# Attention of a decoder trunk: from one block after another to a three-step order with pinned runs

## The chip, the cores and the metric

The kernel runs on one core of a Trainium2 chip. A core has five engines with an instruction queue each: TensorE (PE, matrix products; its weight loads are shown apart as PEld), VectorE (DVE), ScalarE (ACT), GpSimd (POOL) and SyncE (SP, which issues most DMA transfers). An engine works through its queue in order and waits on semaphores where an instruction needs another engine's result. The metric is the time of one execution on the device in microseconds (us), as the median over runs.

## What is computed

A trunk of two layers on a sequence of 1024 tokens of width 1024, in float32. Layer 0 mixes with retention and RWKV-7 heads; layer 1 with sliding-window attention; each is followed by a SwiGLU feed-forward net, and a final RMSNorm ends it. The change is in layer 1's attention (16 query heads in 4 groups, 4 key/value heads, window 128, a learned sink per head):

```python
z = h @ w_qkv + b_qkv
q, k, v = jnp.split(z, [SWA_WIDTH, SWA_WIDTH + SWA_KV_HEADS * HEAD_DIM], axis=-1)
kb, vb = with_prev(k), with_prev(v)        # the block before and this one: 256 keys
s = jnp.einsum('bnqhgd,bnkhd->bnhgqk', q, kb) * HEAD_DIM ** -0.5
s = jnp.where(valid, s, -jnp.inf)
m = jnp.maximum(jnp.max(s, axis=-1, keepdims=True), sink)
e = jnp.exp(s - m)
p = e / (jnp.sum(e, axis=-1, keepdims=True) + jnp.exp(sink - m))
o = jnp.einsum('bnhgqk,bnkhd->bnqhgd', p, vb)
return o.reshape(B, T, SWA_WIDTH) @ w_o + b_o
```

Then `h = h + mix`, a norm, and `(silu(n @ w_gate) * (n @ w_up)) @ w_down`.

## The kernel before

Activations lie transposed: 128 channels on the partitions, tokens along the free axis. The 1024 tokens are two halves of 512 (`hf` 0 and 1); a half is four blocks of 128 tokens. A large product is made from numbers split into a rounded part and its remainder, `hi` and `lo`: three matmuls for each 128x128 weight tile and 512 columns (hi x hi, hi x lo, lo x hi; lines L350 to L352 in `gemm`, L1182 to L1184 in `prod`). `wload` loads a weight (SP queue), ScalarE casts the `hi` part (L335), and VectorE or GpSimd, whichever `K.lo` names at that moment, makes the `lo` part (L336). Split weights lie in a ring of six tiles, each for four of the eight contraction steps; raw weights in a ring of two (`wr`).

Attention of layer 1, for each half:

- `proj` makes 128 channels of queries, keys or values: eight contraction steps, 24 matmuls, into a bank of the PSUM tag `f` (three banks). VectorE scales by the norm's factor (L1496), ScalarE adds the bias (L1497). `kv` calls it four times and copies the keys with their 64-row halves swapped by DMA (`ks`); `queries` calls it four times for each half of the heads.
- `attn` walks 16 blocks, four groups `g` by four token blocks `b`. For a block, `scores` makes four heads' scores of 128 queries by 256 keys: float32 matmuls on 64 rows (L1562), those of two heads side by side on the two halves of the rows, into the tags `r` and `c`. VectorE adds the mask (L1570), takes the maximum (L1576) and does small steps (L1578 to L1580, L1586, L1587); ScalarE takes the exponentials with their sums (L1583); the four heads are scaled by the reciprocal, three on VectorE (L1592), one on ScalarE (L1590).
- `turn` transposes the probabilities with eight 128x128 matmuls against the identity (L1602, tag `m`, two banks); ScalarE and VectorE copy them out (L1604, L1606).
- `out` multiplies by the values: matmuls with 64 columns, two side by side (L1616, tag `y`, one bank). ScalarE and VectorE write `hi` and `lo` parts (L1625, L1626).
- `w_o` is the output projection: eight times 24 matmuls, added to the residual `h` by VectorE (L1642).

The first block of the first half has no block of keys before it, so its scores, transposes and outputs are half as many or half as long, for each of the four groups.

Around it: `norm` of a half is needed for its projections. After `w_o` of the first half, `factor_of` (squares on ScalarE, sums on VectorE, a matmul L373, Ln and Exp) and `form0` (L1130, L358) make the first operands of the feed-forward net, and `ffn_early` makes first products of the gate and up weights for a pair `p` of channel tiles: 48 matmuls, then Silu (L1237) and a product (L1241); its results go to memory by the SP queue (L1246, L1265).

The program is traced in Python in one order; a planner then makes each engine's queue. It simulates the program's time and takes, for a free engine, the ready instruction that was traced first. So later work moves ahead where earlier work isn't ready. Two calls restrict it: `keep(i)` puts an instruction behind the one traced just before it on the same engine; `behind(i, first)` puts it behind a named one. The order of the queues is then fixed. In the kernel before, `attn` uses neither:

```python
for j in range(len(blocks)):
    scores(j, False)
    turn(j)
    out(j, False)
```

and the calls follow as: norm of half 0, keys, values and all queries of half 0; norm of half 1; attention of half 0; keys, values and first queries of half 1; `w_o` of half 0; `form0`; the other queries of half 1; attention of half 1; five pairs of `ffn_early`; `w_o` of half 1. What really interleaves is the planner's choice.

## Time and profile before

| | us |
|---|---|
| three runs, median (lowest to highest) | 2348.12 (2346.57 to 2348.34) |
| the profiled execution, its own time | 2351.35 |
| its span, first to last instruction | 2349.6 |
| first score to last output of both halves | 1432.8 to 1717 in the span |

The granted clock of TensorE was 0.991 on average. In a row of the profile stand the line of the kernel, the engine, the operation, output and inputs by tile name, shapes and a count; then busy time, mean duration, and the idle time ahead of it with what ended it. In a table by stage, each engine has its busy time and in brackets the number of its instructions; then come the clock, the share of DMA and GB/s. A timeline row gives start, duration, engine, line and operation. A float32 matmul is recorded as two instructions, so a block has eight records of scores, eight of transposes and eight of outputs. Busy time of TensorE is modelled from pipelined matmuls; the time between two starts is the surer reading.

### The profile page before, as it was taken

The page shows a single profiled execution, that of the slowest core. Times are in us where ns is not written, and L with a number is a line of the kernel's source. Part 1 is how long each engine was busy: PE and PEld are TensorE (multiplying, and loading weights), DVE is VectorE, ACT ScalarE, POOL GpSimd, SP SyncE. Part 2 cuts the span into 40 slices and gives each one's busy share as a digit, 9 for nine tenths or more (in the row PEclk, how much of TensorE's full clock was granted, in tenths as well). Part 3 has the DMA queues.
Part 4 walks back from the last instruction along what each step waited for, and adds up shares of the span by engine and source line. Part 5 has one row for each costly group of instructions (what it writes and reads, how often), then busy time and mean ns, then how long its engine had stood idle before and what let it go on. Part 6 is the DMA issues. An engine that isn't in the chain of part 4 may idle for free.

```text
span 2349.6 us, 35675 instructions
## 1 busy us (share of the span) xinstructions
PE 2301.8 (98%) x13056; PEld 1822.8 (78%) x13056; DVE 1703.8 (73%) x2667; ACT 1055.7 (45%) x1953; POOL 976.7 (42%) x764
## 2 busy tenths in 40 slices
PE   8999999999999999999999999999999999999998
PEld 6777777777777888888788887777688888887886
DVE  6876765866557548888876876887747788888767
ACT  5354533323555433333333455666735333333335
POOL 3122121211343057777677600002201677776775
PEclk9999999999999999999999999999999999999999
DMA  7565554443345645665685332123236566556763
GB/s 274 199 208 178 180 156 133 131 126 115 126 166 173 208 156 201 216 217 199 231 299 202 126 119 73 51 69 112 93 114 227 172 210 220 212 202 256 257 215 112
DMA packets 170622, 407.46 MB, mean 173 GB/s; under 512 B 43216, under 2 KB 45904, under 8 KB 170448
## 3 DMA queue, kind: packets, MB, share of 16 engines
q1 hardware_dynamic: 167040, 398.63, 49.5%
q10 hardware_dynamic: 2832, 4.45, 0.5%
q8 instruction: 104, 1.70, 0.3%
q0 software_dynamic: 576, 2.10, 0.2%
q14 instruction: 70, 0.57, 0.1%
HBM read 276.53 MB, written 123.21 MB: 170 GB/s over the span
## 4 chain that ended last, share of the span: by engine, by line
PE 75%; DVE 10%; ACT 4%; DMA 4%; issue 4%; POOL 2%; SPq 1%; DVEq 0%; ACTq 0%; POOLq 0%
PE ps_m L1182 7%; PE ps_m L1184 7%; PE ps_m L1183 7%; PE ps_f L240 7%; PE ps_m L240 5%; PE ps_f L350 4%; PE ps_f L352 4%; PE ps_f L351 4%; PE ps_f L1184 4%; PE ps_f L1183 4%; PE ps_f L1182 4%; PE ps_r L1182 2%; PE ps_r L1184 2%; PE ps_r L1183 2%; PE ps_c L1184 2%
## 5 line engine op out<-in xcount | busy, mean ns | idle before, releaser
L240 PE MATMUL ps_f<-n,w 128*128 128x512 f32 x1440 | 387.1, 416 | 10.4 <-ACT w L335 5.7
L240 PEld LDWEIGHTS ps_f<-n,w 128*128 128x128 f32 x1440 | 269.8, 193 | 95.3 <-issue 24.6
L336 POOL TENSOR_TENSOR w<-wr,w 128x512 fp32r<-128x512 f32 x63 | 86.7, 1384 | 524.3 <-ACT w L335 520.6
L335 ACT CAST w<-wr 128x512 fp32r<-128x512 f32 x231 | 141.1, 617 | 181.2 <-PE ps_f L352 70.3
L336 DVE TENSOR_TENSOR w<-wr,w 128x512 fp32r<-128x512 f32 x168 | 119.9, 717 | 56.8 <-ACT w L335 56.3
L336 POOL TENSOR_TENSOR w<-wq,w 128x512 fp32r<-128x512 f32 x91 | 130.4, 1444 | 31.4 <-ACT w L335 31.4
L1182 PE MATMUL ps_m<-n,w 128*128 128x512 f32 x333 | 130.7, 393 | 0.0
L1184 PE MATMUL ps_m<-n,w 128*128 128x512 f32 x333 | 129.8, 390 | 0.4 <-POOL w L1370 0.4
L1183 PE MATMUL ps_m<-n,w 128*128 128x512 f32 x333 | 129.6, 389 | 0.0
L352 PE MATMUL ps_f<-n,w 128*128 128x512 f32 x320 | 126.9, 397 | 0.6 <-POOL w L336 0.6
L350 PE MATMUL ps_f<-n,w 128*128 128x512 f32 x320 | 127.3, 399 | 0.1
L351 PE MATMUL ps_f<-n,w 128*128 128x512 f32 x320 | 126.9, 396 | 0.0
L1191 DVE TENSOR_TENSOR nq<-ps_m,u 128x512 f32<-128x512 f32 x88 | 58.8, 683 | 92.2 <-PE ps_m L1184 92.1
L1182 PE MATMUL ps_f<-n,w 128*128 128x512 f32 x287 | 113.9, 397 | 1.6 <-ACT u L1341 1.6
L1184 PE MATMUL ps_f<-n,w 128*128 128x512 f32 x287 | 112.1, 392 | 0.0
L1183 PE MATMUL ps_f<-n,w 128*128 128x512 f32 x287 | 111.8, 389 | 0.0
L358 POOL TENSOR_TENSOR n<-nq,n 128x512 fp32r<-128x512 f32 x60 | 100.0, 1679 | 7.6 <-ACT n L356 7.6
L1370 POOL TENSOR_TENSOR w<-wd,w 128x512 fp32r<-128x512 f32 (+1 forms) x62 | 85.9, 1393 | 39.6 <-ACT w L1369 37.9
L1182 PE MATMUL ps_m<-cb,w 128*128 128x512 f32 x236 | 91.9, 390 | 0.3 <-DVE nq L1191 0.3
L1183 PE MATMUL ps_m<-cb,w 128*128 128x512 f32 x236 | 91.8, 389 | 0.0
L1184 PE MATMUL ps_m<-cb,w 128*128 128x512 f32 x236 | 91.8, 389 | 0.0
L1370 POOL TENSOR_TENSOR w<-ws,w 128x512 fp32r<-128x512 f32 (+1 forms) x48 | 71.3, 1491 | 47.0 <-ACT w L1369 43.5
(520 smaller groups left out, 6472.9 us busy)
## 6 DMA issues: line engine op xcount, KB each, us to landing
hc<-n SPq DMA_DIRECT2D x84, 512.0 KB, 2.9
wsp<-w SPq DMA_DIRECT2D x54, 512.0 KB, 3.4
w<-wsp SPq DMA_DIRECT2D x54, 512.0 KB, 3.7
n<-hc SPq DMA_DIRECT2D x54, 512.0 KB, 5.7
wq<-in_w_gate SPq DMA_DIRECT2D x44, 512.0 KB, 4.4
u<-u SPq DMA_DIRECT2D x88, 256.0 KB, 2.9
wr<-in_w_in SPq DMA_DIRECT2D x34, 512.0 KB, 5.2
ha<-hc SPq DMA_DIRECT2D x34, 512.0 KB, 5.6
```

The lines of the kernel that those rows point to most:

```text
L240: self.nc.tensor.matmul(out, lhsT, rhs, **kw)
L335: nc.scalar.copy(hi[:, :n], raw[:, c])
L336: self.lo.tensor_tensor(out=lo[:, :n], in0=raw[:, c], in1=hi.bitcast(F32)[:, :n], op=ALU.subtract)
L350: nc.tensor.matmul(ps, hi, rh, start=k == 0, stop=False)
L351: nc.tensor.matmul(ps, hi, rl, start=False, stop=False)
L352: nc.tensor.matmul(ps, lo, rh, start=False, stop=k == n - 1)
L358: e.tensor_tensor(out=lo, in0=src, in1=hi.bitcast(F32), op=ALU.subtract)
L1182: mm(ps, hi, xh, start=first and k == 0, stop=False, skip_group_check=True)
L1183: mm(ps, hi, xl, start=False, stop=False, skip_group_check=True)
L1184: mm(ps, lo, xh, start=False, stop=last and k == len(w) - 1, skip_group_check=True)
L1191: self.last_add = V.tensor_tensor(out=o, in0=x, in1=y, op=ALU.add)
L1370: nc.gpsimd.tensor_tensor(out=lo, in0=v, in1=hi.bitcast(F32), op=ALU.subtract)
```

## The change

`attn` becomes a generator of 19 steps. Step `j` holds the transposes of block j-2, the outputs of block j-3 and the scores of block j, in this order; outputs and scores are each kept behind the matmul traced before, from the point where three blocks are on the way. Behind the scores come the step's fills, whose first matmul is put behind the last matmul of the step before. A fill is a half of a projection (12 matmuls), as `proj`, `kv` and `queries` now yield after four of the eight contraction steps; in the second half it is a half of a gate/up pair (24 matmuls). The first scaling of the four heads goes from VectorE to GpSimd.

The order of calls: only four of half 0's query projections precede its attention; the other four fill steps 0 to 2, half 1's keys and values steps 3 to 8, and five of half 1's query projections steps 9 to 17. Then come the first two steps of half 1's attention, `w_o` of half 0, its third step, `form0`, half 1's last three query projections, and the other steps with the five gate/up pairs as fills.

```diff
+    def pinned(self, x):
+        if self.pin is not None:
+            self.behind(x, self.pin)
+            self.pin = None
...
     def proj(self, nr, ti, out, **kw):
...
-        self.gemm(ps, w, nr[0])
+        for k in (0, 4):
+            self.prod(ps, w[k : k + 4], nr[0][k : k + 4], k == 0, k == 4)
+            if k == 0:
+                yield
...
-                    V.tensor_scalar(
+                    (nc.gpsimd if h == 0 else V).tensor_scalar(
...
-        for j in range(len(blocks)):
-            scores(j, False)
-            turn(j)
-            out(j, False)
-        return [self.hl(n8, k) for k in range(KT)]
+        n = len(blocks)
+        for j in range(n + 3):
+            if 0 <= j - 2 < n:
+                turn(j - 2)
+            if 0 <= j - 3 < n:
+                n8 = n8 or outs()
+                out(j - 3, j - 2 < n)
+            if j < n:
+                scores(j, j >= 3)
+            for f in fill.get(j, ()):
+                self.pin = last
+                f()
+                self.pin = None
+            last = self.tail
+            self.ch[hf] = n8 and [self.hl(n8, k) for k in range(KT)]
+            yield
...
-        kv = K.kv(0, n0, ap)
-        q = [x for j in range(2) for x in K.queries(n0, ap, j)]
+        run(K.kv(0, n0, ap))
+        q0 = K.queries(0, n0, ap)
+        for _ in range(8):
+            next(q0)
         n1 = K.norm(K.kt(K.h[1]), "n1b", K.n8(nb), ap)
-        c0 = K.attn(0, kv, q, ap, K.n8(K.pp))
-        kv = K.kv(1, n1, ap)
-        q = K.queries(n1, ap, 0)
-        K.w_o(0, c0)
+        kv, q1 = K.kv(1, n1, ap), K.queries(1, n1, ap)
...
+        fill = {j: [take(q0)] * n for j, n in enumerate((4, 2, 2))}
+        fill |= {j + 3: [take(kv)] * n for j, n in enumerate((1, 1, 2, 1, 1, 2))}
+        fill |= {j + 9: [take(q1)] * n for j, n in enumerate((1, 1, 1, 1, 1, 2, 1, 1, 1))}
...
+        g = pairs()
+        run(K.attn(0, ap, lambda: K.n8(K.pp), fill))
+        a1 = K.attn(1, ap, lambda: K.n8(nb), {j: [take(g)] for j in (4, 5, 6, 8, 9, 10, 12, 13, 14, 16)})
+        next(a1)
+        next(a1)
+        K.w_o(0, K.ch[0])
+        next(a1)
         gs, sp = K.pool("sp", "left")
         K.form0("n2b", K.factor_of(0, sp), K.n8(K.pp), sp)
-        q += K.queries(n1, ap, 1)
-        c1 = K.attn(1, kv, q, ap, K.n8(nb))
-        K.lo = tc.nc.gpsimd
-        early(1, sp, 0, 5)
+        run(q1)
+        run(a1)
         K.lo = tc.nc.vector
-        K.w_o(1, c1)
+        K.w_o(1, K.ch[1])
```

`gemm` and `prod` call `pinned` on their first matmul; `pairs()` yields each gate/up pair in two halves, with `K.lo` on GpSimd while a pair's weights are split; `ffn_early` yields between its halves.

More of the change, by code (lines that the diff above doesn't have):

```diff
@@ L1181, in prod @@
         for k, ((hi, lo), (xh, xl)) in enumerate(zip(w, x)):
-            mm(ps, hi, xh, start=first and k == 0, stop=False, skip_group_check=True)
+            i = mm(ps, hi, xh, start=first and k == 0, stop=False, skip_group_check=True)
+            self.pinned(i)
             mm(ps, hi, xl, start=False, stop=False, skip_group_check=True)
@@ L1514, in kv @@
             ks.append(st)
[L1515 removed]
+            yield
         if hf:
[L1517 to L1521 removed]
+            G.tensor_copy(vt[:, 0, :], pvt[:, 4, :])
+        for i in range(2):
+            vc = self.t(self.pp, [P, HT], "nq", 4)
+            yield from self.proj(nr, 10 + i, vc, bias=self.col("bqkv", 10 + i))
             pt = self.pst("m", [P, 4, P])
@@ L1746, in early @@
                 K.lo = tc.nc.vector if form else tc.nc.gpsimd
-                K.ffn_early(L, p, sp, "ff" if L and p < 6 else "fm")
+                run(K.ffn_early(L, p, sp, "ff" if L and p < 6 else "fm"))
                 K.lo = tc.nc.gpsimd
```

62 lines of the change are left out of this document (40 added, 22 removed).

## The prediction

> **What bounds the kernel now.** I read the page first: engines, clock, the chain that ended last.
>
> ```profile
> span 2349.6 us, 35675 instructions
> PE 2301.8 (98%) x13056; PEld 1822.8 (78%) x13056; DVE 1703.8 (73%) x2667; ACT 1055.7 (45%) x1953; POOL 976.7 (42%) x764
> PEclk9999999999999999999999999999999999999999
> PE 75%; DVE 10%; ACT 4%; DMA 4%; issue 4%; POOL 2%; SPq 1%; DVEq 0%; ACTq 0%; POOLq 0%
> ```
>
> TensorE (PE) is busy in 98% of the span and the clock never drops, so only PE time can be won. But the page says that ends of matmuls are modelled: a busy PE can still issue late. So the second view is a table by stage, with instructions counted (the number after x), for the four stages around the change: first half's attention, its output projection, second half's attention, its output projection. The same table for scores (L1562), transposes (L1602) and outputs (L1616) follows, for the two attention stages.
>
> ```profile
> 1432.00:1560.00 128.00, 126.47 (x700) 87.52 (x699) 109.51 (x287) 88.44 (x271) 0.00 (x0) 1.00 0.15 47
> 1560.00:1610.00 50.00, 50.00 (x221) 40.76 (x221) 36.61 (x67) 28.15 (x57) 5.46 (x4) 1.00 0.38 131
> 1610.00:1718.00 108.00, 106.51 (x579) 76.12 (x580) 73.32 (x156) 68.81 (x177) 22.02 (x17) 1.00 0.28 99
> 1718.00:1762.00 44.00, 44.00 (x196) 36.40 (x195) 19.96 (x29) 16.01 (x27) 5.16 (x4) 1.00 0.32 108
> ...
> 1432.00:1560.00 128.00, 29.66 (x176) 17.51 (x176) 1.00 0.15 47
> 1610.00:1718.00 108.00, 13.40 (x80) 8.05 (x80) 1.00 0.28 99
> ...
> 1432.00:1560.00 128.00, 21.10 (x136) 15.61 (x136) 1.00 0.15 47
> 1610.00:1718.00 108.00, 16.60 (x104) 11.86 (x104) 1.00 0.28 99
> ...
> 1432.00:1560.00 128.00, 15.84 (x112) 6.53 (x112) 1.00 0.15 47
> 1610.00:1718.00 108.00, 17.24 (x128) 7.65 (x128) 1.00 0.28 99
> ```
>
> The projection stages run at 44/196 = 50/221 = 0.225 us per matmul; with an instruction counted at each edge I use 0.226. The third view is the timeline of PE around one block (start, duration).
>
> ```profile
> 1498.54 0.60 PE L1602 MATMUL ps_m<-c_ident,s 128*128 128x128 f32 x4
> ...
> 1500.13 0.40 PE L350 MATMUL ps_f<-n,w 128*128 128x512 f32 x1
> 1500.46 1.08 PE L1616 MATMUL ps_y<-pT,vt 128*64 128x256 f32 x8
> 1501.47 0.48 PE L1562 MATMUL ps_c<-ks,q 64*128 64x256 f32 x1
> ...
> 1501.79 0.38 PE L1562 MATMUL ps_c<-ks,q 64*128 64x256 f32 x1
> ...
> 1502.01 0.38 PE L1562 MATMUL ps_c<-ks,q 64*128 64x256 f32 x1
> ...
> 1502.53 0.50 PE L351 MATMUL ps_f<-n,w 128*128 128x512 f32 x1
> 1502.87 0.40 PE L352 MATMUL ps_f<-n,w 128*128 128x512 f32 x1
> ```
>
> Scores and outputs run as pairs side by side, a pair per 0.215 us (1501.79 to 1502.01; I take the same for outputs), so four pairs of either need 0.86 us. A transpose takes (0.60 - 0.28)/3 = 0.107 us (0.28 is one's own length). From the matmul at 1500.13 to the one at 1502.87 there are 2.74 us, for 0.226 + 0.86 + 0.86 + 0.226 = 2.17 of work. The other 0.57 go to three changes of form (128x128 to 64 columns, to 64 rows, and back): **0.19 us per change**.
>
> Now the loss by stage. First half: 700 instructions less 176, 136, 112, eight transposes of values and two of a norm leave 266 full matmuls, 60.1 us; scores 72 x 0.215 + 16 half-long pairs x 0.12 = 17.4; 144 transposes 15.4; outputs 56 x 0.215 = 12.0; norm 0.9. That is 105.8 of 128: 22.2 lost. Second half: 267 x 0.226 + 40 x 0.215 + 104 x 0.107 + 64 x 0.215 = 93.8 of 108: 14.2 lost. Together **36.4 us** are lost, and next to nothing elsewhere in the four stages.
>
> Following the timeline between the first score and the last output, I count 42 runs of scores and 33 of outputs (for 32 blocks), nine directly behind one another, and 141 changes of form.
>
> ```profile
> L1562 PE MATMUL ps_c<-ks,q x64: 272/376/480, 1432.8 to 1646.8; 64*128 64x256 f32 x56, 64*128 64x128 f32 x8
> L1616 PE MATMUL ps_y<-pT,vt x240: 379/379/431, 1448.4 to 1717.0; 128*64 128x256 f32 x120
> L1590 ACT ACTIVATE s<-s,st x32: 399/508/517, 1439.6 to 1691.4; 128x256 f32<-128x256 f32 x28, 128x128 f32<-128x128 f32 x4
> 1512.89 0.49 ACT L1590 ACTIVATE s<-s,st 128x256 f32<-128x256 f32 x1
> ...
> 1676.49 0.70 PE L1562 MATMUL ps_c<-kc,q 64*128 64x256 f32 x2
> ```
>
> 141 x 0.19 = 26.8 us. The remaining **9.6 us** I read as waits, mostly on the softmax.
>
> **The change part by part.**
>
> *Pinned runs (gain 7.4).* In each half 16 blocks take 19 steps. Steps 0 and 1 have scores alone (2 changes each), step 2 transposes and scores (2), steps 3 to 15 all three (3 each), steps 16 to 18 outputs at most (2 each): 4 + 2 + 39 + 6 = 51, so 102 for both halves, 19.4 us against 26.8. Lower bound of the gain: if fills fall between outputs and scores, 64 runs make 128 changes, 24.3 us, gain 2.5. Transposes may mix with full matmuls at no cost: they have the same form.
>
> *The wait that the pin adds.* Transposes of block j stand two steps behind its scores, and behind them on PE are queued outputs, scores and the next fill. A full step of the first half is 0.86 + 0.86 + 0.86 + 0.57 = 3.15 us plus 16 fills of twelve matmuls (2.71) over 13 steps, 3.34: 6.49. Scores start about 1.96 (transposes, outputs, two changes) after the step, so the softmax has 2 x 6.49 - 1.96 = 11.0 us. Today it takes, from the first score to the last scaling, 1513.4 - 1501.5 = 11.9 for that block and 1440.0 - 1432.8 = 7.2 for the first (half as long, alone). At 11.9 a step becomes 6.93 and 13 steps lose 5.7; near 7 they lose nothing. In the second half ten fills of 24 matmuls (5.42) make the step 7.32 and leave 12.7; the last block there takes 1691.9 - 1676.5 = 15.4, which would make it 8.68 and lose 17.7. There the softmaxes ran one behind the other, so much of the 15.4 is queueing that later scores would remove. So waits lie between 0 and 23.4 us. I take 5, near the low end, because the 11.9 misses its allowance by under 1 us, fills not pinned behind this step's scores can go ahead of late transposes, and weights of the next fills are split ahead. Against today's 9.6 this gains 4.6.
>
> *One of three scalings to GpSimd.*
>
> ```profile
> L1592 DVE TENSOR_SCALAR s<-s,st 128x256 f32<-128x256 f32 (+1 forms) x96 | 30.3, 371 | 0.2
> L1517 POOL COPY vt<-vt 128x256 f32<-128x256 f32 x1 | 0.6, 622 | 15.3 <-ACT vt L1525 15.3
> 1636.75 1.92 DVE L1592 TENSOR_SCALAR s<-s,st 128x256 f32<-128x256 f32 x3
> 1637.25 1.27 POOL L336 TENSOR_TENSOR w<-wr,w 128x512 fp32r<-128x512 f32 x1 [4.27 <-ACT w L335]
> ```
>
> VectorE loses 30.3/3 = 10.1 us of work; GpSimd gains 32 x 0.62 (its copy of the same shape) = 20, on an engine that did nothing in the first half and 22 of 108 us in the second. It is on no path if it runs beside the other two. The last two rows say it may not: three scalings took 1.92 us while GpSimd worked 1.27, where three alone take 3 x 0.316 = 0.95 (30.3/96 each). Bounds on the softmax: 0.3 shorter to 0.62 + 0.63 - 0.95 = 0.3 longer, or longer still behind a 1.27 us split; I take no change.
> The Trainium skill, "SBUF — State Buffer", section "Who interferes with whom", says that a tensor_scalar on VectorE can hold the port pair that it shares with GpSimd, and that the one that comes second is blocked for the whole instruction. The 1.92 us agrees. By it the sum would be 0.3/2 x 13 = 2 us less gain in the first half; by the row of two engines side by side, none.
>
> *Fills in halves, moves.* The number of matmuls, weight loads and their DMAs is unchanged; only places change. The first half's last four query projections, the second half's keys and values and five of its eight query projections go into the first half's steps; five gate/up pairs into the second's.
>
> ```profile
> L336 DVE TENSOR_TENSOR w<-wr,w 128x512 fp32r<-128x512 f32 x29 | 19.9, 686 | 12.3 <-ACT w L335 12.2
> wr<-in_w_qkv SPq DMA_DIRECT2D x14, 512.0 KB, 3.3
> SPq L1246 <- DVE sg L1241: 54.6, 5, 14.0
> L1130 DVE SCALAR_TENSOR_TENSOR u<-h,pv,rs 128x512 f32<-128x512 f32 x8 | 6.6, 870 | 4.0 <-ACT rs L375 4.0
> L358 DVE TENSOR_TENSOR n<-u,n 128x512 fp32r<-128x512 f32 x8 | 8.3, 1072 | 0.0
> L1237 ACT ACT_TABLE_LOAD x4 | 5.1, 1283 | 0.1
> ```
>
> A fill brings VectorE one split (0.69) ahead of time; its cover is the ring of six weight tiles. Without it each late split costs up to 0.69 us. Loads land in 3.3 us and a fill comes every 3 to 6, but the SP queue is in order and has stood up to 14.0 us behind a pair's write; six tiles are six fills, over 16 us, so I cost it at nothing. The second keys' swapped copy waits in that queue for the first half's scores; its readers come after the output projection. The pairs' activations alternate with exponentials: up to ten table loads where the stage has four and three back, three more, 3.9 us on ScalarE, which is busy 68.8 of 108: hidden; if not, 3.9 on the path.
> Second half's first scores ahead of the output projection: nothing on PE itself. But behind that projection the norm's chain and 8 x (0.87 + 1.07) = 15.5 us on VectorE must pass before the first pair; with the chain I put it at 20. The cover is the six remaining fills (16.3), step 2 (about 2.3) and step 3 (3.15), 21.7: nothing, and up to 4 where softmaxes come between. It is inside the waits' bounds.
>
> **Sum.** 36.4 - 19.4 - 5 = 12.0 us gained. Against the profiled execution's own 2351.35 us this is 2339.4; that run lies 3.2 above the median 2348.12, so against the median it is **2336**.
>
> **Rivals.** *Full gain.* The softmax fits everywhere and waits vanish: gain 17.0, 2331. For it: VectorE still had 18 us idle of 128. Against: VectorE is at 86% there and the order is fixed ahead of time.
> *The softmax distance (slower).* The two steps between a block's scores and its transposes are too short for the softmax, and PE waits the whole 23.4: 36.4 - 19.4 - 23.4 = -6.4, 2354.5. It decides above 17.0 us of waits, that is about 0.65 us in each of 26 full steps. For it: 15.4 us of the last block, and VectorE's in-order waits. Against: fills enough to cover, 11.9 in the first half.
> *It does not do what it says.* The planner that orders instructions puts halves of fills between outputs and scores (only scores and outputs are pinned to what is traced before them, and fills only behind the last step): 128 changes and waits as now, gain 2.5, 2345.6. For it: today's order splits 32 blocks into 75 runs. Against: the pins leave it few places.
>
> **How the numbers follow.** Forecast (2332.5 to 2343) 0.49, full gain 0.18, not doing it 0.13, softmax distance 0.20. What a measurement can tell from no change is 0.2%, 4.7 us. Faster is forecast and full gain, 0.67; same 0.13; slower 0.20. The range goes from 2330, just below the full gain, to 2354, where half of the slower case is left out.
>
> **What would show it.** Right: the two attention stages with the same instructions lose some 24 us in place of 36; scores directly behind outputs in 26 blocks, hence 64 runs and about 102 changes; PE rows of the timeline never further apart than 0.5 us; L1592 twice on VectorE and once on GpSimd per block. Wrong: waits of the transposes on the last scaling (VectorE, GpSimd or ScalarE) of 0.65 us and more at each step, GpSimd's scaling over 1 us, TensorE waiting for a weight split in a fill, or a hole before the first gate/up pair.

## The result, and the profile after

The changed kernel takes 2344.47 us (median of 22 runs, 2338.92 to 2350.74) where the kernel before takes 2348.61 (22 runs, 2344.42 to 2354.38). The ratio is 0.9981, with a 95% interval of 0.9974 to 0.9989: a gain of 4.4 us (2.6 to 6.1). It is real, since the interval leaves out 1, and it lies at the bound of 0.2% that the prediction set for no change. The forecast was a gain of 12.0.

The page of the changed kernel, its span, busy times and the engines of the chain that ended last:

```profile
span 2343.4 us, 35741 instructions
PE 2290.0 (98%) x13056; PEld 1817.0 (78%) x13056; DVE 1697.9 (72%) x2635; ACT 1060.1 (45%) x1956; POOL 1004.2 (43%) x796
...
PE 76%; DVE 10%; ACT 5%; DMA 4%; issue 3%; SPq 1%; POOL 1%; DVEq 0%; ACTq 0%; POOLq 0%
```

TensorE is the bound as before, with the same 13056 matmuls. The profiled run took 2345.18 us; the spans differ by 6.2 us. From the timeline, TensorE's 7100th instruction (first layer, ahead of the stages in question) starts at 1028.4 us before and at 1025.6 after; from there to the 11000th it takes 837.8 and 832.5. So 2.8 us of the 6.2 come from stages that the change does not touch and are no part of its effect, 5.3 come from the stages that it does touch, and 1.9 are lost again behind them. The granted clock of TensorE differs outside these stages: ahead of 1028 us it stood at one half for 34.1 us in the trace before and 20.5 after, and behind them the changed kernel has 3.4 us of it at 2129.6 where the kernel before has none. Between 1372 and 1772 us neither has any.

The stretch from 1372 to 1772 us holds both attention stages and both output projections in either kernel. The table by stage has, after the window and its length, the busy time and the count (x) of TensorE, its weight loads, VectorE, ScalarE and GpSimd, then the granted clock, the DMA share and GB/s. Before:

```profile
1372.00:1772.00 400.00, 396.98 (x2000) 298.38 (x1999) 273.86 (x590) 239.90 (x588) 33.84 (x27) 1.00 0.28 93
```

After:

```profile
1372.00:1772.00 400.00, 394.13 (x2023) 300.37 (x2022) 272.09 (x567) 246.35 (x598) 63.36 (x59) 1.00 0.29 96
```

What counts is x: 23 more matmuls in the same 400 us, although "busy" fell from 396.98 to 394.13. In either kernel 758 instructions of the stretch are the same: 256 scores (25.8 us by their spacing in the timeline), 240 attention transposes (26.1), 240 outputs (25.6), 16 transposes of values (1.7) and 6 of the norm (2.6), together 81.8; two more are cut by the edges, and the rest are full matmuls at 0.2267. So the loss of the stretch (its length less this work) is close to 400 - 81.8 - (x - 760) x 0.2267; counted from the timeline it is 37.0 us before and 31.8 after. The gain there is 5.2.

From the timeline I count in this stretch the changes of form (as the prediction did: between 128x128 matmuls, those on 64 rows and those with 64 columns), and as waits all that a start comes later than is usual for its pair of kinds, where that is over 0.06 us. The kernels of the study by the same count (o_price, which adds work, is told below):

| kernel | changes of form | runs of scores / outputs | waits, us | loss, us | median, us | ratio to before (95%) |
|---|---|---|---|---|---|---|
| before | 141 | 42 / 33 | 5.4 | 37.0 | 2348.61 | 1 |
| after | 108 | 35 / 32 | 7.9 | 31.8 | 2344.47 | 0.9981 (0.9974-0.9989) |
| a_dve | 109 | 36 / 32 | 10.7 | 35.3 | 2345.70 | 0.9991 (0.9980-1.0002) |
| b_bank | 105 | 34 / 32 | 13.2 | 39.6 | 2353.47 | 1.0019 (1.0008-1.0030) |
| c_both | 102 | 32 / 32 | 12.0 | 36.6 | 2345.68 | 0.9989 (0.9978-1.0001) |
| d_between | 125 | 32 / 32 | 50.1 | 77.3 | 2388.09 | 1.0170 (1.0156-1.0184) |
| e_old_pool | 156 | 51 / 33 | 3.0 | 37.2 | 2351.69 | 1.0017 (1.0007-1.0028) |
| f_nopin | 147 | 50 / 37 | 2.3 | 38.3 | 2350.99 | 1.0017 (1.0007-1.0028) |
| g_dist3 | 119 | 38 / 32 | 13.4 | 40.4 | 2352.33 | 1.0023 (1.0013-1.0034) |
| h_pair | 94 | 36 / 18 | 12.0 | 36.4 | 2348.09 | 0.9998 (0.9985-1.0010) |
| k_runs | 104 | 35 / 31 | 10.1 | 33.5 | 2343.51 | 0.9981 (0.9971-0.9992) |
| l_fills | 144 | 43 / 41 | 1.7 | 37.2 | 2350.10 | 1.0006 (0.9995-1.0017) |
| n_pairruns | 99 | 40 / 17 | 3.7 | 29.1 | 2341.70 | 0.9970 (0.9958-0.9981) |

In six of these kernels the granted clock stood at one half for a part of the stretch, and their loss, in part also their waits, holds what that cost, estimated as half of TensorE's busy time there: a_dve, c_both and h_pair 1.7 us each (3.4 us of half clock), b_bank 3.0 (6.8), g_dist3 6.5 (13.7), d_between 17.8 (41.0). The other seven have none.

Changes fell by 33. What is left of the loss once the waits are taken off is 31.6 / 141 = 0.224 us per change before and 23.9 / 108 = 0.221 after. The loss thus splits into 7.7 us won on changes and 2.5 us given back in waits. Over all thirteen kernels the same remainder is 0.22 to 0.26 us per change, so the split holds to a few us and no better.

The timeline of the changed kernel around one step (start, duration, engine and line; in brackets the idle time and what ended it):

```profile
1496.58 0.39 PE L1191 MATMUL ps_f<-n,wx 128*128 128x512 f32 x1
...
1498.00 1.09 PE L1621 MATMUL ps_m<-c_ident,s 128*128 128x128 f32 x8 [1.03 <-POOL s L1611]
1499.02 1.08 PE L1635 MATMUL ps_y<-pT,vt 128*64 128x256 f32 x8
1500.04 0.37 PE L1580 MATMUL ps_c<-kc,q 64*128 64x128 f32 x1
...
1500.68 0.50 PE L1188 MATMUL ps_f<-n,wx 128*128 128x512 f32 x1
```

Both halves of the result stand here. Transposes, eight outputs and eight scores come in one run, as the change says, with three changes of form. And the first transpose starts 1.42 us after a matmul that holds TensorE for 0.23: a wait of 1.19, which the view puts down to GpSimd's scaling.

That scaling did end last, at 1497.94, but VectorE's two of the same block ended only 0.3 us sooner, at 1497.63. All of them started late, since VectorE came late to the reciprocal that they need:

```profile
1495.39 0.16 DVE L1605 TENSOR_TENSOR st<-st 128x4 f32<-128x4 f32 x1
1495.47 1.21 DVE L1595 TENSOR_REDUCE st<-s 128x4 f32<-128x1024 f32 x1
1496.60 0.17 DVE L1606 RECIPROCAL st<-st 128x4 f32<-128x4 f32 x1
```

Between the sum (L1605) and the reciprocal (L1606) of the block that TensorE waits for stands the maximum of the next block (L1595). From sum to reciprocal it is 1.21 us, where it is 0.20 with nothing in between. Something stands there in 13 of the 32 blocks, 0.86 us on average; at the other wait put down to GpSimd (1630.7) it is 0.69. The softmax of this block took 12.2 us from its first score (1485.78), 1.2 more than the 11.0 that the prediction allowed. No run changed VectorE's order alone, so what this order is worth is not shown.

TensorE's waits in the stretch as the profile attributes them (tile and line that waited, what it waited for, us, times, longest). Before:

```profile
PE ps_c L1562 <- DVE st L1586: 1.1, 1, 1.1
PE ps_y L1616 <- DVE n L1626: 0.7, 2, 0.6
PE ps_m L1602 <- ACT s L1583: 0.5, 1, 0.5
PE ps_r L1562 <- DVE s L1570: 0.4, 1, 0.4
```

After:

```profile
PE ps_m L1621 <- ACT vt L1541: 2.1, 2, 1.3
PE ps_m L1621 <- POOL s L1611: 2.1, 2, 1.0
PE ps_m L1621 <- ACT pT L1623: 0.6, 1, 0.6
PE ps_m L1621 <- DVE pT L1625: 0.4, 1, 0.4
PE ps_m L1621 <- ACT s L1609: 0.4, 1, 0.4
PE ps_m L1621 <- DVE s L1611: 0.2, 1, 0.2
```

2.7 us became 5.8 (this view counts only time in which the engine is idle, so it is lower than my count; the difference, 3.1 against 2.5, is much the same). And they moved: before, scores and outputs waited for the most part (2.2 of 2.7); after, all waits are those of the transposes (L1621): 2.7 on the scalings and 3.1 on a free bank (copies of values, L1541, and of transposed probabilities, L1623 and L1625).

### The profile page after: what moved, and what is told of

Same layout as the page of the kernel before. It is cut to its first block, busy times and chain, and to the rows that moved or that the text cites. A ratio compares the mean times of both kernels' runs of the same rounds, so it can differ in the third digit from the quotient of the medians.

```text
span 2343.4 us, 35741 instructions
## 1 busy us (share of the span) xinstructions
PE 2290.0 (98%) x13056; PEld 1817.0 (78%) x13056; DVE 1697.9 (72%) x2635; ACT 1060.1 (45%) x1956; POOL 1004.2 (43%) x796
## 4 chain that ended last, share of the span: by engine, by line
PE 76%; DVE 10%; ACT 5%; DMA 4%; issue 3%; SPq 1%; POOL 1%; DVEq 0%; ACTq 0%; POOLq 0%
PE ps_f L240 8%; PE ps_m L1188 7%; PE ps_m L1191 7%; PE ps_m L1190 7%; PE ps_f L1188 5%; PE ps_f L1190 5%; PE ps_m L240 5%; PE ps_f L1191 5%; PE ps_r L1188 2%; PE ps_r L1190 2%; PE ps_r L1191 2%; PE ps_c L1191 2%; PE ps_c L1190 2%; PE ps_c L1188 2%; PE ps_f L353 2%
## 5 line engine op out<-in xcount | busy, mean ns | idle before, releaser
L240 PE MATMUL ps_f<-n,w 128*128 128x512 f32 x1440 | 384.4, 414 | 10.1 <-ACT w L335 6.1
L240 PEld LDWEIGHTS ps_f<-n,w 128*128 128x128 f32 x1440 | 267.5, 191 | 94.4 <-issue 23.6
L1188 PE MATMUL ps_f<-n,w 128*128 128x512 f32 x415 | 164.8, 397 | 1.6 <-ACT u L1349 1.6
L1190 PE MATMUL ps_f<-n,w 128*128 128x512 f32 x415 | 163.3, 393 | 0.1
L1191 PE MATMUL ps_f<-n,w 128*128 128x512 f32 x415 | 162.4, 392 | 0.0
L1611 POOL TENSOR_SCALAR s<-s,st 128x256 f32<-128x256 f32 (+1 forms) x32 | 30.1, 942 | 208.5 <-DVE st L1606 55.6
L1378 POOL TENSOR_TENSOR w<-wd,w 128x512 fp32r<-128x512 f32 (+1 forms) x62 | 86.0, 1394 | 40.4 <-ACT w L1377 37.0
L1188 PEld LDWEIGHTS ps_f<-n,w 128*128 128x128 f32 x415 | 77.8, 188 | 23.0 <-issue 4.7
L1190 PEld LDWEIGHTS ps_f<-n,w 128*128 128x128 f32 x415 | 77.9, 188 | 19.1 <-issue 2.9
```

What stands on the lines that cost most here:

```text
L240: self.nc.tensor.matmul(out, lhsT, rhs, **kw)
L1188: i = mm(ps, hi, xh, start=first and k == 0, stop=False, skip_group_check=True)
L1190: mm(ps, hi, xl, start=False, stop=False, skip_group_check=True)
L1191: mm(ps, lo, xh, start=False, stop=last and k == len(w) - 1, skip_group_check=True)
L1378: nc.gpsimd.tensor_tensor(out=lo, in0=v, in1=hi.bitcast(F32), op=ALU.subtract)
L1611: (nc.gpsimd if h == 0 else V).tensor_scalar(out=s[:, h, kw], in0=s[:, h, kw], scalar1=den[:, h : h + 1], scalar2=None, op0=ALU.mult)
```

## Experiments

The theory in the end: the gain is the changes of form, at about 0.2 us each, and most of the rest of the forecast was lost because pinned runs make TensorE stand still where before another instruction went first. Its rivals: one late supplier (GpSimd's slow scaling, or the bank) makes the new waits, and with it gone the forecast's gain comes; the two steps between scores and transposes are too few; changes of form are worth little, and both the loss and the gain are waits.

### One late supplier: a_dve, b_bank, c_both

a_dve has all scalings that are not ScalarE's on VectorE:

```
-                    (nc.gpsimd if h == 0 else V).tensor_scalar(
+                    V.tensor_scalar(
```

> The changed kernel with all three scalings back on VectorE. My theory now: in the two attention stages TensorE loses 31.8 us, 108 changes of form at 0.22 and 7.9 us of waits; 2.4 of these are transposes waiting for GpSimd's scaling (1.19 at 1496.6, 1.18 at 1629.3), because one takes 0.94 us there against 0.42 on VectorE. Then the loss falls to about 29.4 and the time by 2 us against the changed kernel. Rival: GpSimd relieves VectorE, which gets 10 us of work back; the softmax grows longer, waits stay at 8 us or grow, and the time is the same or up to 3 us longer.

b_bank turns the values in the projections' banks, so that the transposes of the attention do not wait for the copy of the values:

```
-            pt = self.pst("m", [P, 4, P])
+            pt = self.pst("f", [P, 4, P])
```

> The changed kernel with the four value transposes of each half's second fills in a bank of the three-bank tag f in place of the two-bank tag m. My theory: the waits of 1.44 at 1470.3 and 1.03 at 1477.7 are attention transposes for which no bank of m is free until ScalarE, behind four exponentials, has copied the values out; without them the loss falls by 2.5 to 29.3 and the time by 2.5 us. Rival: the softmax of that block isn't ready any sooner, and the wait comes back under another name: loss 31 to 32, time the same.

c_both has both edits.

> Both edits: scalings on VectorE and value transposes in the other tag. If the two waits are independent: loss 31.8 - 4.9 = 26.9, time 5 us below the changed kernel and 9 to 10 below the kernel before (ratio 0.996). If waits only change their names: loss about 31, time as the changed kernel.

The table by stage of a_dve:

```profile
1372.00:1772.00 400.00, 393.21 (x2008) 298.67 (x2007) 272.06 (x592) 244.56 (x595) 33.25 (x27) 1.00 0.28 95
```

Of b_bank:

```profile
1372.00:1772.00 400.00, 388.16 (x1988) 295.93 (x1988) 266.88 (x555) 240.87 (x589) 63.83 (x59) 0.99 0.28 92
```

Neither gains: 2008 and 1988 matmuls against the 2023 of the changed kernel, and c_both has 1999. TensorE's waits of c_both show why:

```profile
PE ps_m L1621 <- DVE s L1611: 3.7, 4, 1.4
PE ps_f L1540 <- ACT nq L1510: 3.4, 2, 1.9
PE ps_f L1188 <- ACT u L1349: 1.0, 1, 1.0
PE ps_f L350 <- ACT sg L1244: 1.0, 1, 1.0
PE ps_m L1621 <- ACT s L1609: 0.8, 1, 0.8
PE ps_m L1621 <- DVE pT L1625: 0.7, 1, 0.7
```

The wait for the copy of the values is gone, and so is GpSimd's; in their place the value transposes wait for their own operand (L1540), full matmuls for theirs, and the same transposes for VectorE's scaling. c_both even reaches the 102 changes of the forecast and has 12.0 us of waits. The rival of one late supplier falls in this form: the waits for each are in the list of the changed kernel, but with a supplier taken away TensorE waits elsewhere. Since an edit makes the planner place every later instruction anew, these runs do not say what one wait alone would be worth.

### Where the fills stand: d_between

The fills stand between a step's outputs and its scores, which costs one change of form more in each step:

```
-            if j < n:
-                scores(j, j >= 3)
+            if j < 3:
+                scores(j, False)
             for f in fill.get(j, ()):
-                self.pin = last
+                self.pin = self.tail if j >= 3 else last
                 f()
                 self.pin = None
+            if 3 <= j < n:
+                scores(j, True)
```

> The changed kernel with the fills of steps 3 to 15 put between outputs and scores in place of behind the scores: nothing is added but changes of form, one more pair of changes less one joint in each of 26 steps, 26 changes. My theory, 0.22 us per change: loss 31.8 + 5.7 = 37.5, time 5.7 us longer than the changed kernel, slower than the kernel before by 1. Rival: the stages are bound by the softmax and the changes of form are in the shadow of its waits: loss and time within 1.5 us of the changed kernel.

Measured: 125 changes, 17 more than the changed kernel, and 2388.09 us, 44 more. At 0.22 the changes are 3.7 us. The count of gaps rose from 7.9 to 50.1, but not all of that is waits: the profile lists 31.5 us of them (5.8 in the changed kernel), and about 18 are the half clock behind the longer ones, which stood for 41.0 us of the stretch. The first row of TensorE's waits of this kernel:

```profile
PE ps_m L1621 <- POOL s L1611: 20.9, 7, 5.1
```

The table by stage:

```profile
1372.00:1772.00 400.00, 368.57 (x1823) 272.12 (x1822) 245.35 (x528) 223.91 (x559) 58.54 (x55) 0.95 0.24 79
```

With the fills between outputs and scores, a step's scores come directly ahead of the next step's transposes. That does two things at once: nothing is left to work on when the transposes are late, and the softmax, which starts at the scores, has the length of a fill less time (2.7 or 5.4 us by the prediction's sizes). The run does not tell these apart. Either way a fill's place behind the scores is worth far more than the change of form that it saves, and the expectation, which priced little more than the changes, missed it.

### Which pin does it: f_nopin, k_runs, l_fills

The changed kernel has two kinds of pins: scores and outputs held in the order in which they are written (the runs), and a step's fills held behind the last run. f_nopin has neither, k_runs the first alone, l_fills the second alone:

```
f_nopin:
-                out(j - 3, j - 2 < n)
+                out(j - 3, False)
...
-                scores(j, j >= 3)
+                scores(j, False)
...
-                self.pin = last
+                self.pin = None
k_runs:
-                self.pin = last
+                self.pin = None
l_fills:
-                out(j - 3, j - 2 < n)
+                out(j - 3, False)
...
-                scores(j, j >= 3)
+                scores(j, False)
```

> The changed kernel's steps, fills and order of calls, but nothing pinned. In its queue of TensorE the two attention stages have 147 changes of form (changed kernel 108, before 141). Theory of the changes at 0.22 us: loss 147 x 0.22 = 32.3 and waits as in the changed kernel, 7.9: 40 in place of 31.8, time 8 us above the changed kernel, ratio to the kernel before about 1.001. Rival: the pins are what makes TensorE wait; free of them it waits 5 us or less and gives back part: loss 37, time 5 above. Second rival, the order of steps and fills is what gained and the pins nothing: time as the changed kernel.

> The changed kernel with the runs pinned (outputs behind transposes, scores behind outputs) and the fills free. 104 changes of form in the queue. Without any pin the two stages lost 147 x 0.22 and 2.3 us of waits; with both pins 108 x 0.22 and 7.9. If the run's pin makes the waits (TensorE stands before a transpose with outputs, scores and next fills queued behind it): waits of 6 to 10, loss 29 to 33, time within 2 us of the changed kernel, ratio to before 0.9970 to 0.9990. If the fills' pin makes them: waits of 2 to 4, loss 26, time 6 us below the changed kernel, ratio 0.9955.

> The changed kernel with the fills pinned behind the last step and the runs free. 144 changes of form in the queue. If the run's pin makes the waits: waits of 2 to 4, loss 144 x 0.22 + 3 = 35, time 3 us above the changed kernel. If the fills' pin makes them: waits of 6 to 8, loss 39, time 7 us above it, ratio to before 1.001.

The tables by stage; f_nopin:

```profile
1372.00:1772.00 400.00, 398.71 (x1994) 298.20 (x1993) 265.01 (x557) 242.17 (x591) 63.38 (x59) 1.00 0.27 93
```

k_runs:

```profile
1372.00:1772.00 400.00, 391.04 (x2015) 299.45 (x2014) 273.15 (x568) 244.97 (x596) 64.32 (x59) 1.00 0.28 95
```

l_fills:

```profile
1372.00:1772.00 400.00, 398.78 (x1999) 297.39 (x1998) 265.02 (x557) 243.06 (x592) 62.93 (x59) 1.00 0.28 94
```

TensorE's waits of f_nopin, all of them:

```profile
PE ps_y L1635 <- DVE n L1646: 0.7, 1, 0.7
PE ps_f L1188 <- ACT u L1349: 0.4, 1, 0.4
PE ps_f L1190 <- DVE n L364: 0.2, 1, 0.2
```

Of k_runs, its three longest:

```profile
PE ps_m L1621 <- POOL s L1611: 2.9, 4, 1.1
PE ps_f L350 <- ACT n L1645: 2.1, 2, 1.6
PE ps_m L1621 <- ACT pT L1623: 1.3, 1, 1.3
```

The four kernels make a square. Pinning the runs takes 43 changes away without the fills' pin (147 to 104) and 36 with it (144 to 108), and adds 7.8 and 6.2 us of waits (2.3 to 10.1, 1.7 to 7.9). It makes both, the gain and the new waits: outside the waits the loss falls by 12.6 and 11.6 us, the waits take back 7.8 and 6.2, and the net is 4.8 and 5.4 us of loss. (43 and 36 changes at 0.2 are only 8.6 and 7.2; what the other 4 us are was not found.) The pin of the fills does nothing here that can be told: 0.9981 with and without it, and 1.0006 against 1.0017 with overlapping intervals. And the new order of the calls by itself, without pins, gives no gain: f_nopin has 147 changes, more than before, and is slower (1.0007 to 1.0028).

The two kernels with free runs read "busy" 398.7 and 398.8 of 400 and do fewer matmuls than the pinned ones at 391.0 and 394.1: where the planner may choose, TensorE has nearly no waits (2.3 and 1.7 us) and the runs are split for it.

### GpSimd's scaling alone: e_old_pool

In the kernel before, the first scaling of each block goes to GpSimd:

```
-                    V.tensor_scalar(
+                    (nc.gpsimd if h == 0 else V).tensor_scalar(
```

> The kernel before with the one edit that the first of its four scalings goes to GpSimd. 156 changes of form in the queue in place of 141. Theory: 15 more changes cost 3.3 us, and GpSimd's scaling at 0.94 us adds up to 2 us of waits: time 3 to 5 us above the kernel before, ratio 1.0015. Rival: relieving VectorE by 10 us shortens the softmax and waits: time the same or 2 us below.

```profile
1372.00:1772.00 400.00, 398.90 (x1999) 297.23 (x1998) 264.72 (x559) 239.59 (x590) 63.56 (x59) 1.00 0.28 94
```

This table by stage has 1999 matmuls where the kernel before has 2000: the edit brings these stages nothing (156 changes, 15 more; 3.0 us of waits, 2.4 fewer; loss 37.2). The time is nevertheless longer, 1.0007 to 1.0028 of before. The profile cannot show where: the execution that was profiled took 2350.59 us, no more than that of the kernel before (2351.35), and from TensorE's 7100th to its 11000th instruction it takes 837.9 us, against 837.8. That stays open, and with it how much of f_nopin's equal ratio is this edit.

### A step more of distance: g_dist3

Transposes three steps behind their scores instead of two, outputs four; the scores' tiles get a fourth buffer, and the transposed probabilities give one up:

```
-            s = sm[j] = self.t(ap, [P, 4, 256], "s", 3)
+            s = sm[j] = self.t(ap, [P, 4, 256], "s", 4)
-            pT = pTs[j] = self.t(ap, [P, 2, 4, P], "pT", 3)
+            pT = pTs[j] = self.t(ap, [P, 2, 4, P], "pT", 2)
-        for j in range(n + 3):
-            if 0 <= j - 2 < n:
-                turn(j - 2)
+        for j in range(n + 4):
             if 0 <= j - 3 < n:
+                turn(j - 3)
+            if 0 <= j - 4 < n:
                 n8 = n8 or outs()
-                out(j - 3, j - 2 < n)
+                out(j - 4, j - 3 < n)
             if j < n:
-                scores(j, j >= 3)
+                scores(j, j >= 4)
```

> The changed kernel with transposes three steps behind the scores in place of two, outputs four (20 steps; four buffers for scores, two for transposed probabilities, which take the same room). 119 changes of form in the queue. If the remaining waits come from the softmax's distance: waits fall from 7.9 to under 3, loss 26.2 + 3 = 29, time 2 to 3 us below the changed kernel in spite of 11 more changes. Rival: the waits come from what the planner's simulated time has wrong (order fixed ahead, banks, copies, weights), wherever the transposes stand: waits 8 to 12, loss 34 to 38, time 2 to 6 us above the changed kernel.

TensorE's waits, all of them:

```profile
PE ps_y L1635 <- DVE n L1646: 3.1, 2, 2.7
PE ps_f L1190 <- DVE n L364: 1.9, 1, 1.9
PE ps_m L1621 <- ACT vt L1541: 1.3, 2, 0.7
```

The waits on scalings are gone from the list, as a longer distance should make them, but the total is not lower: 6.3 us in place of 5.8 (13.4 by my count, some 6 of them half clock). The changes are 119, and the kernel is slower than before. Outputs wait for a free bank behind VectorE's second pass over the last result, up to 2.7 us. So a longer distance alone did not bring the gain; but the run also gave up a buffer of the transposed probabilities, so it does not rule out that a third step with all buffers would do better. That was not tried.

### Fewer changes still: h_pair, n_pairruns

Every second step does the outputs of two blocks into one bank, copied out together, which saves two changes of form every second step. h_pair keeps both pins, n_pairruns leaves the fills free:

```
-            if 0 <= j - 3 < n:
+            if j >= 4 and j % 2 == 0:
                 n8 = n8 or outs()
-                out(j - 3, j - 2 < n)
+                po = self.pst("y", [P, 2, 2, P])
+                out(j - 4, j - 2 < n, po[:, :, 0])
+                out(j - 3, True, po[:, :, 1])
...
+                S.copy(hi, po)
+                V.tensor_tensor(out=lo_, in0=po, in1=hi.bitcast(F32), op=ALU.subtract)
n_pairruns, besides:
-                self.pin = last
+                self.pin = None
```

> The changed kernel with the outputs of two neighbouring blocks together in every second step, written out with one copy and one subtraction in place of two. 94 changes of form in the queue in place of 108. Theory of the changes: loss 94 x 0.22 = 20.7 and waits of 8: 28.7, time 3 us below the changed kernel, ratio to before 0.997. Rival: waits, not changes, set the time; they move with any reordering by several us, and the time is anywhere within 5 us of the changed kernel.

> Outputs of two blocks together, in every second step, runs pinned and fills free: 99 changes of form in the queue. In the paired kernel with both pins one wait of 2.19 us was followed by 3.4 us at a granted clock of 0.5, and the loss was 36.4. If free fills take the waits away: waits of 3, loss 25, time 7 us below the changed kernel, ratio to before 0.995. If the run's pin makes them: waits of 8 to 12 and perhaps a half clock, loss 30 to 36, ratio 0.998 to 1.000.

The tables by stage; h_pair:

```profile
1372.00:1772.00 400.00, 391.13 (x2002) 299.32 (x2001) 267.62 (x543) 242.59 (x575) 66.80 (x59) 1.00 0.28 93
```

n_pairruns:

```profile
1372.00:1772.00 400.00, 396.44 (x2035) 305.70 (x2034) 278.40 (x559) 246.22 (x584) 63.76 (x59) 1.00 0.30 99
```

h_pair has the fewest changes of all, 94, and no gain over the kernel before (0.9985 to 1.0010): waits are 12.0. n_pairruns has 99 and 3.7, does the most matmuls of all in the stretch, 2035, and is the fastest: 0.9970 (0.9958 to 0.9981). It beats the kernel before; against the changed kernel (0.9974 to 0.9989) the intervals overlap, so it is the better one by the profile (loss 29.1 against 31.8) and not surely by the time. Here the fills' pin mattered, in the other direction than meant: without it the waits fell from 12.0 to 3.7 us, and the two intervals do not overlap. The changes saved by the pairs show no gain: outside the waits h_pair loses 24.4 us (1.7 of them half clock) and n_pairruns 25.4, against 23.9 of the changed kernel with its 108 changes and 23.4 of k_runs with 104. What n_pairruns wins over these two it wins in waits. Why its changes go with more loss each, 0.26 us, was not found.

### The price of a change of form: o_price

To tell whether the changes or only waits are worth something, the price was measured by itself: 32 small matmuls on 64 rows (of keys, into a bank nobody reads) stand between the full matmuls of the second half's output projection, which waits for nothing.

```
-            self.gemm(ps, w, ch)
+            for k in range(0, KT, 2):
+                self.prod(ps, w[k : k + 2], ch[k : k + 2], k == 0, k == 6)
+                if hf:
+                    x = self.akv[1][0][0]
+                    pm = self.pst("m", [P, P])
+                    self.keep(nc.tensor.matmul(pm, x[0:64, 0:P], x[0:64, P : 2 * P], start=True, stop=True))
```

> The price of a change of form by itself, away from the softmax: the changed kernel with 32 small float32 matmuls on 64 rows (keys against keys, 128 columns, result unread) set between the full matmuls of the second half's output projection. In the queue they stand in 28 places, which makes 56 more changes. Each is 0.12 us of work. Theory, 0.22 us per change wherever it stands: 32 x 0.12 + 56 x 0.22 = 16.2 us on the projection stage and on the time, slower than the kernel before by 12. Rival: what I called the price of a change is waits of the attention stages in small pieces; then it costs the work alone, 4 us, and the time equals the kernel before.

The timeline of TensorE around one of them (each leaves two instructions, x2):

```profile
1738.00 0.39 PE L1191 MATMUL ps_f<-n,w 128*128 128x512 f32 x1
1738.32 0.48 PE L1676 MATMUL ps_m<-kc 64*128 64x128 f32 x2
1738.73 0.50 PE L1188 MATMUL ps_f<-n,w 128*128 128x512 f32 x1
1739.07 0.39 PE L1190 MATMUL ps_f<-n,w 128*128 128x512 f32 x1
```

From 1738.00 to 1739.07 there are 1.07 us, for two full matmuls, 0.45: the insertion cost 0.62. All 26 isolated insertions cost 0.61 to 0.63. The planner also put some together: four instructions in a row cost 0.84 and eight 1.39, so one instruction's own work is (0.84 - 0.62)/2 = 0.11 to (1.39 - 0.84)/4 = 0.14. That leaves 0.34 to 0.40 for the two changes of an insertion, 0.17 to 0.20 each. The 28 places cost 18.3 us in the trace, and the median rose to 2363.49 (four runs; 19 above the changed kernel). The rival of waits alone falls: a change of form costs about the prediction's 0.19 with no wait near it. Nor is it the price of any small matmul put in between: transposes, which have the form of the full matmuls and write another bank, stand between full matmuls in ten places of the stretch in the kernel before, and cost 0.01 to 0.03 us beyond their own work. Changes to and from 64 columns were not measured alone. The Trainium skill, "TensorEngine Tiling (Array Packing)", section "Key Properties", says that changing the tiling mode drains TensorE; a cost at each change, 0.62 us a place, agrees, and that page gives no figure for it.

## Why the prediction came out as it did

The forecast was 2336 us and the time is 2344.47. The direction and the gain from fewer changes of form were right; the term for the waits had the wrong sign.

- **What bounds the kernel.** Right. TensorE is the bound, and the gain is where its changes of form are fewer. "The clock never drops" is too much said: the slices of the page are too wide to show stretches of half clock, of which the trace before has over 40 us in all, though none in the stages in question.
- **0.19 us per change.** Right as the price of the change itself (0.17 to 0.20). But in the attention stages of these two kernels each change goes with 0.22 us once the waits are off. What the other 0.02 to 0.05 are was not found. It sets the split of the loss: 26.8 + 9.6 in the prediction, 31.6 + 5.4 by the count of gaps. There was thus less waiting to win than the prediction believed.
- **Pinned runs: 141 to 102 changes, gain 7.4.** Nearly right: 108 changes, gain 7.7. All 26 full steps have scores behind outputs. The six missing changes are three runs of scores too many, at 1486, 1526 and 1532 us: one block of the first half is split 2 and 6, and the second half's first blocks, which have no pin, are split among fills.
- **The wait that the pin adds: "I take 5", 4.6 gained against today's 9.6.** This is the step that failed. Waits went from 5.4 to 7.9 by gaps, or 2.7 to 5.8 by the profile's attribution: a loss of 2.5 to 3.1 where a gain of 4.6 stood. The range of 0 to 23.4 held, but the chosen value was set against waits that were read off as a remainder, and not counted. And the term had the softmax's distance alone: of the 5.8 us in the profile's list 3.1 are waits for a bank. The reasons given for the low end did not suffice: fills did go ahead of late transposes (the 12 matmuls from 1493.95 are the fill of the step whose transposes start at 1498.00), and TensorE waited 1.19 us all the same. In the square of four kernels, pinning the runs adds 6.2 to 7.8 us of waits. (The time from a step's start to its scores, 1.96, is short by the prediction's own terms, which make 2.10; the changed kernel has 1.98, from 1503.54 to 1505.52.)
- **GpSimd at 0.62 us per scaling, no change.** The size was wrong and the consequence right. Groups of instructions of the changed kernel (busy us, mean ns):

```profile
L1611 POOL TENSOR_SCALAR s<-s,st 128x256 f32<-128x256 f32 (+1 forms) x32 | 30.1, 942 | 208.5 <-DVE st L1606 55.6 <-ACT pT L1623 39.6 <-ACT w L335 27.4
...
L1611 DVE TENSOR_SCALAR s<-s,st 128x256 f32<-128x256 f32 (+1 forms) x64 | 24.1, 419 | 0.5
```

  The scaling took 0.94 us on average over both shapes, and VectorE's own rose from 371 to 419 ns, so VectorE saved 30.3 - 24.1 = 6.2 us and not 10.1. All the same a_dve, without it, is at 0.9980 to 1.0002, which overlaps the changed kernel: the transposes wait for VectorE instead. VectorE's scalings of 128 x 256 took 0.34 us where GpSimd did nothing, and up to 0.59 beside GpSimd's scaling. Of the rule that the prediction weighed (the Trainium skill, "SBUF — State Buffer", section "Who interferes with whom"), the trace agrees in sign and not in size: none of them stood for the length of GpSimd's scaling, which is 0.92 us or more at this shape. The 2 us that it would have cost are not visible in a_dve.
- **Fills in halves and second half ahead of the projection: nothing.** Right for the pin of the fills (k_runs, l_fills). No hole stands before the first gate/up pair of the changed kernel: no wait of a full matmul is in its list. ScalarE's table loads, taken as hidden, may not all be: the waits of 0.77 us at 1622.9 and 0.57 at 1660.8 are for ScalarE's work, which runs late behind loads of 1.28 us at 1618.99 and 1657.41. No run took these away. Without pins the new order of the calls, with GpSimd's scaling, is 0.17% slower than before, which the prediction did not see; e_old_pool shows as much with the scaling alone, and the two profiles place at most 1.3 us of it in these stages.
- **The rivals.** The time is next to the one of "it does not do what it says" (2345.6), but not by its mechanism: it needed 128 changes, and 26 of 26 runs were joined. That the time fell there is chance, and alone it would have pointed to the wrong cause. The softmax distance needed 17 us of waits, 0.65 us in each of 26 steps; there are seven waits of 0.57 us or more, 6.8 us together. Waits of this kind did eat gain, but all waits together are 7.9 us, less than half of what that rival needs.
- **Sum.** 7.7 - 2.5 = 5.2 us in the stretch in place of 12.0. With the 1.9 lost again behind it the two profiles show 3.3, and the ratio of the times 4.4 (2.6 to 6.1).

What stays open is why each new wait stands where it does. That the planner orders by its own estimate of durations, and a pinned run turns an error of that estimate into a wait, would fit these runs, and VectorE's work for a later block ahead of a reciprocal that TensorE waits for as well; but it is argued, and no run changed the estimates alone.

## What to carry to other kernels

Count the waits before you plan to win them: a loss that is left over after one cause is priced belongs to every cause that was priced too low. Holding matmuls of one form together won 12 us outside the waits here, but an order held in place also gives up the instructions that used to stand in for late ones, and 6 to 8 us went back into waits. So try which part of the order has to be held: with outputs in pairs, freeing the fills took the waits from 12.0 to 3.7 us and made the fastest kernel (0.9970). Look also at the other engines' order: a wait that is put down to the last supplier can begin further up its chain. A busy share of TensorE near 100% is no sign of little loss: the three kernels with the highest share (398.7 to 398.9 of 400) did 1994 to 1999 matmuls where the changed kernel did 2023 at 394.1.

## What was not expected of the hardware

**A wait of about 2 us can cost more than itself.** In several runs the granted clock fell to one half around a wait of TensorE. Stretches of b_bank around one of 3.4 us that began at 1630.3:

```profile
1630.00:1634.00 4.00, 0.73 (x4) 0.27 (x2) 3.43 (x9) 2.36 (x7) 2.27 (x2) 0.91 0.17 66
1634.00:1640.00 6.00, 5.93 (x16) 4.66 (x17) 1.18 (x4) 2.88 (x11) 2.28 (x2) 0.50 0.40 134
```

And of h_pair behind one of 2.19 us that began at 1670.3:

```profile
1673.00:1676.00 3.00, 2.93 (x12) 2.26 (x11) 1.18 (x4) 1.96 (x6) 2.25 (x2) 0.67 0.23 87
```

The clock (third column from the end) is 0.50 through the whole second stretch of b_bank. By the clock's events in the traces, such a slow stretch lasts 3.41 us or a multiple: 1674.0 to 1677.4 in h_pair, 1633.3 to 1640.1 in b_bank, 1651.5 to 1661.8 after a wait of 2.77 us in g_dist3. In these stages it begins from some 2 us ahead of the end of a wait to 2 us behind it (both in d_between).

The length of the wait does not decide it alone. The same wait for the same operand stands in b_bank and in c_both (idle time in brackets):

```profile
1388.09 0.66 PE L1540 MATMUL ps_f<-c_ident,nq 128*128 128x128 f32 x4 [1.85 <-ACT nq L1510]
...
1393.97 0.87 PE L1540 MATMUL ps_f<-c_ident,nq 128*128 128x128 f32 x4 [1.85 <-ACT nq L1510]
```

In b_bank (the first row) the clock stays at full; in c_both it is one half from 1394.3 to 1397.7, and the same four transposes take 0.87 us in place of 0.66. In d_between one begins ahead of the end of a wait with 1.44 us of idle time. So no threshold comes out of these runs. In the stages in question every wait with more than 1.9 us of idle time had a slow stretch near its end, and the changed kernel's longest, 1.28 us of idle time, had none. So it costs the changed kernel nothing there, and it is one reason why the variants with longer waits did worse than their waits. The Trainium skill, "TensorE: Matmul & The Clock Gate", section "What's actually happening", tells of half clock after an idle window of about 3.4 us that runs freely; the length of the slow stretches agrees, but here an idle time of 1.85 us, in c_both, could be enough.

**GpSimd's scaling** of 128 x 256 values took 0.92 to 1.38 us, 0.99 on average over 28, where its copy of the same shape, from which its price was taken, took 0.61 and 0.62 (one in each kernel). The four scalings of 128 x 128 took 0.60 to 0.65, so a copy's time is no price for a scaling.
